# Second feed-forward block: gate and up projections as seven block products, interleaved with the down projection in three chunks

## The chip, the cores and the metric

The kernel runs on one core of a Trainium2 chip. The metric is the time of one execution in device microseconds (us), the median of three runs. The core has a matrix engine (TensorE, PE in the profile), a vector engine (VectorE, DVE), a scalar engine (ScalarE, ACT), GpSimd (POOL), and a queue (SyncE, SP) from which all loads and stores are issued here.

## The reference

One residual block on 512 tokens of width 1024, in float32: a half-step SwiGLU feed-forward block (FFN), a mixer of a gated DeltaNet group and a latent attention group, and a second half-step FFN. The change is in the second FFN, which computes

```
h  = rms(x) * (1 + scale) + shift            # scale and shift from the condition c, one per channel
gate, up = split(h @ w_in)                   # w_in: 1024 x 5632, so gate and up have 2816 columns each
x  = x + 0.5 * g * ((silu(gate) * up) @ w_out)   # w_out: 2816 x 1024
```

## The kernel before

Activations lie transposed: a tile has 128 channels on the partitions and 512 tokens in the free dimension. x is eight such tiles, `self.xT[0..7]`. Each number that goes through TensorE is split in a high part (rounded to the format fp32r) and a low part (the rest), and each product is three matmuls (`mm3`, L257 to L261): high weight by high data (L259), high weight by low data (L260), low weight by high data (L261).

Weights come in units (`unit`, L198): one load of 8 x 128 x 128 numbers (512 KB; 6 x 128 x 128, 384 KB, for the last part of a down column) into a raw tile `wr`, a cast on ScalarE into the high tile `wh` (L191) and a subtraction on VectorE into the low tile `wl` (L192). Each of the three kinds has four tiles (pool `wp`, `bufs=4`, L83). A tile is given out again when its last reader has finished. `plan_units` lists the units in order; `next_unit` hands out the next and starts one more.

Other tiles of 128 x 512 come from a pool of 56 slots. In PSUM, where TensorE writes, there are three accumulators from `acc` (named pa) and five from `aux` (named pb).

The second FFN is `ffn2` (L718). `first_units` does three units (gate and up of column tile 0, gate of column tile 1) in two halves of 256 tokens, since the normalised input h of the second half is still being made. After that each of the 22 column tiles takes a gate unit and an up unit of 24 matmuls of 512 tokens each (8 input tiles by three), and `glu` (L585) makes the product: Silu on ScalarE, a multiplication, a cast to the high part (L592) and a subtraction for the low part (L593). When all 22 are there, `down` (L645) makes the eight output tiles: 22 input tiles by three matmuls each, in three units, and adds the result to x (L652). The last output tile is done in two halves of 256 tokens. `store` transposes a finished tile back on TensorE (L712), copies it (L714) and writes it out.

The order of the work on TensorE is the order of the program. Where code runs under `in_order` (L131), every engine, SP and GpSimd included, executes its instructions in the order in which the program emits them.

The input h of the second FFN is made in `norm_half` and `modulate` (L439 to L457), per half of the tokens: a multiplication on VectorE (L452), an addition of the shift with rounding on ScalarE (L454), and the low part on VectorE (L446). The late pool (12 more slots, used by the first FFN's last results) is closed by `late_exit` at the very end.

Of the kernel before, what the change touches and what calls it, by code (L numbers as in the profile page):

```python
# [18 lines left out]
P = 128  # L19
# [8 lines left out]
KPARTS = ((0, 8), (8, 8), (16, 6))  # L28

# [48 lines left out]
class Block:  # L78
# [144 lines left out]
    def plan_units(self):  # L223
# [4 lines left out]
        def ffn(w1, w2, first, ts):  # L228
            for f in range(first, FT):
                cols(w1, f * P)  # L230
                cols(w1, DFF + f * P)
            for t in ts:
                for k0, n in KPARTS:
                    self.specs.append(lambda k0=k0, n=n, t=t: self.unit(w2[k0 * P:(k0 + n) * P, t * P:(t + 1) * P], n))

        ffn(ins["ffn1_w_in"][0], ins["ffn1_w_out"][0], 3, [*range(KT), KT - 2])
# [10 lines left out]
        ffn(ins["ffn2_w_in"][0], ins["ffn2_w_out"][0], 0, range(KT))  # L247
# [168 lines left out]

    def rstd_diag(self, v):

        return self.diag(self.rms_cols(v, v.shape[1], D))
# [52 lines left out]
    def norm_half(self, half, acc, j):  # L472
# [5 lines left out]
        for k in range(0, KT, 2):  # L478
            self.modulate(range(k, k + 2), ts, rb, self.mod[j + 1], self.mod[j])
            yield  # L480

    def first_units(self, n, nb, lead, marks):
# [5 lines left out]
        with self.matmuls_in_order(self.last_mm):  # L488
            for half in range(2):
                ts = slice(half * HALF, half * HALF + HALF)  # L490
                for at, (kt, i) in enumerate([(kt, i) for kt in range(KT) for i in range(n)] if half else first):
                    self.dense(ps[i], units[i], self.h, ts, kt, kt + 1)
# [152 lines left out]
    def down(self, act, gate, norm=None):  # L645

        nc = self.nc
        accum = self.slot(s="na") if norm else None
        full, ha, hb = slice(0, NT), slice(0, HALF), slice(HALF, NT)

        def finish(t, ts, p):
            nc.vector.scalar_tensor_tensor(out=self.xT[t][:, ts], in0=p[:, ts], scalar=gate[:, t:t + 1],  # L652
                                           in1=self.xT[t][:, ts], op0=ALU.mult, op1=ALU.add)
            if norm:
                self.square_in(t, ts, accum)
# [12 lines left out]
        last = KT - 2 if norm else KT - 1  # L668
        side = Side()
        if norm:  # L670
            side.add(self.ada_rest((2, 3), True))
        for t in range(last):
            if norm and t == 1:
                self.masks()
            for i, _ in enumerate(parts(t, full)):
                side.step((2, 1, 2)[i])
                if not norm and i == 1 and t > 0:
                    self.store(t - 1, range(NB))
        side.flush()
        if not norm:  # L680
            t = KT - 1
            units = [self.next_unit(ahead=0) for _ in KPARTS]
            for i, _ in enumerate(parts(t, ha, units)):
                if i == 1:
                    self.store(t - 1, range(NB))
            for i, _ in enumerate(parts(t, hb, units)):
                if i == 1:
                    self.store(t, range(2))
            self.store(t, range(2, 4))
            return None  # L690
# [27 lines left out]
    def ffn2(self, nb):  # L718
        act = []
        ps = self.first_units(3, nb, 2, (7, 18, 15))  # L720
# [1060 lines left out]
```

## Time and profile before

| | |
|---|---|
| three runs | 1093.94, 1094.52, 1096.87 us; median 1094.52 |
| span of the profiled execution | 1091.4 us (the page gives no other time of it; the median of the runs stands 3.1 us above) |
| busy over the span | TensorE 97%, VectorE 52%, ScalarE 35%, GpSimd 4% |
| mean granted TensorE clock | 0.989 of full speed |
| second FFN | its first matmul starts at 717.1 us; to the end |

The span runs from the first to the last instruction of one profiled execution. Matmuls are pipelined: one starts before the one ahead of it has ended, so their durations overlap and the distance of starts is what one costs. A line such as L191 or L259 belongs to a helper and stands for all its callers; the names of the tiles (`wh<-wr`, `pa<-hh,wh`) tell them apart. `x60` is a count, the number behind the busy time is the mean in ns, and behind the last bar stands the idle time of the engine ahead of these instructions with what ended it.

### The profile page before, as it was taken

Reading aid. Unit: us, or ns where it says so; the run is one execution under the profiler, and the core shown is the slowest. Engines: PE = TensorE matmul, PEld = TensorE weight load, DVE = VectorE, ACT = ScalarE, POOL = GpSimd, SP = SyncE. Lnnn points to the kernel's source line nnn. Section 1 sums busy time; section 2 is a strip of 40 time slices with the busy share of each in tenths; the row PEclk is TensorE's granted clock in tenths of the full one; section 3 lists DMA queues with packets and bytes.
Section 4 is the critical chain, followed back from the end, with each engine's and each line's share of the span. In section 5 each row is a group of like instructions: output and inputs, shape, how many; then the busy total and the mean of one; then the engine's idle time right before and its main releaser. Section 6 shows DMA issues by size and latency. Waiting matters only on the chain. (4 is left out here: it accounts for less than half of the span.)

```text
span 1091.4 us, 14122 instructions
## 1 busy us (share of the span) xinstructions
PE 1059.7 (97%) x5583; PEld 880.8 (81%) x5583; DVE 571.5 (52%) x1021; ACT 385.6 (35%) x636; POOL 43.2 (4%) x94
## 2 busy tenths in 40 slices
PE   6999999999999999998997999999999999999998
PEld 4778878788887899886776779988888888888887
DVE  4488884333687366388767545684333333322220
ACT  4242222222222235475565434443222222222220
POOL 1000000000000000001000021200000000000000
PEclk9999999999999999999999969999999999999999
DMA  9989963332796455221223001124333333334320
GB/s 275 268 244 302 295 202 97 96 97 87 241 289 218 115 127 151 59 58 39 59 54 82 6 20 40 39 78 116 97 97 97 97 97 97 92 97 115 97 72 30
DMA packets 210576, 132.04 MB, mean 121 GB/s; under 512 B 13633, under 2 KB 194638, under 8 KB 210510
## 3 DMA queue, kind: packets, MB, share of 16 engines
q1 hardware_dynamic: 210510, 131.14, 41.2%
q8 instruction: 44, 0.72, 0.3%
q14 instruction: 22, 0.18, 0.1%
HBM read 128.63 MB, written 2.49 MB: 120 GB/s over the span
## 5 line engine op out<-in xcount | busy, mean ns | idle before, releaser
L191 ACT CAST wh<-wr 128x1024 fp32r<-128x1024 f32 (+1 forms) x170 | 173.3, 1021 | 494.8 <-PE pa L260 338.3
L259 PE MATMUL pa<-hh,wh 128*128 128x512 f32 (+1 forms) x885 | 338.6, 383 | 5.5 <-ACT z L1597 4.3
L260 PE MATMUL pa<-hl,wh 128*128 128x512 f32 (+1 forms) x885 | 336.5, 380 | 3.3 <-DVE hl L446 3.2
L261 PE MATMUL pa<-hh,wl 128*128 128x512 f32 (+1 forms) x885 | 336.0, 380 | 0.0
L192 DVE TENSOR_TENSOR wl<-wr,wh 128x1024 fp32r<-128x1024 f32 (+1 forms) x170 | 201.5, 1186 | 237.5 <-ACT wh L191 231.4
L259 PEld LDWEIGHTS pa<-hh,wh 128*128 128x128 f32 x885 | 166.8, 188 | 40.5 <-ACT z L1597 4.7
L260 PEld LDWEIGHTS pa<-hl,wh 128*128 128x128 f32 x885 | 166.8, 188 | 34.7 <-DVE hl L446 4.6
L261 PEld LDWEIGHTS pa<-hh,wl 128*128 128x128 f32 x885 | 166.7, 188 | 30.8 <-DVE wl L192 0.4
L259 PE MATMUL pa<-ah,wh 128*128 128x512 f32 (+1 forms) x418 | 150.1, 359 | 0.0
L261 PE MATMUL pa<-ah,wl 128*128 128x512 f32 (+1 forms) x418 | 148.8, 356 | 0.0
L260 PE MATMUL pa<-al,wh 128*128 128x512 f32 (+1 forms) x418 | 148.6, 356 | 0.0
L259 PEld LDWEIGHTS pa<-ah,wh 128*128 128x128 f32 x418 | 79.0, 189 | 12.7 <-ACT wh L191 1.7
L261 PEld LDWEIGHTS pa<-ah,wl 128*128 128x128 f32 x418 | 79.0, 189 | 11.4
L260 PEld LDWEIGHTS pa<-al,wh 128*128 128x128 f32 x418 | 79.0, 189 | 11.0
L590 DVE TENSOR_TENSOR af<-sg,pa 128x512 f32<-128x512 f32 x40 | 27.5, 687 | 103.0 <-PE pa L261 102.9
L544 DVE SCALAR_TENSOR_TENSOR aa<-ar,sc,aa 128x512 f32<-128x512 f32 x98 | 73.2, 751 | 14.3 <-DMA ar<-in_w_ada 12.9
L652 DVE SCALAR_TENSOR_TENSOR xT<-pa,mod,xT 128x512 f32<-128x512 f32 (+1 forms) x19 | 12.7, 667 | 48.3 <-PE pa L261 48.3
L592 ACT CAST ah<-af 128x512 fp32r<-128x512 f32 x44 | 27.4, 622 | 19.3 <-DVE af L590 19.3
L259 PE MATMUL pa<-mh,wh 128*128 128x256 f32 (+1 forms) x96 | 32.6, 341 | 0.0
L260 PE MATMUL pa<-ml,wh 128*128 128x256 f32 (+1 forms) x96 | 32.3, 336 | 0.0
L261 PE MATMUL pa<-mh,wl 128*128 128x256 f32 (+1 forms) x96 | 32.0, 333 | 0.0
L593 DVE TENSOR_TENSOR al<-af,ah 128x512 fp32r<-128x512 f32 x44 | 30.2, 687 | 1.0 <-ACT ah L592 0.9
(350 smaller groups left out, 985.5 us busy)
## 6 DMA issues: line engine op xcount, KB each, us to landing
wr<-in_ffn_w_in SPq DMA_DIRECT2D x82, 512.0 KB, 3.9
ar<-in_w_ada SPq DMA_DIRECT2D x48, 512.0 KB, 6.6
wr<-in_ffn_w_out SPq DMA_DIRECT2D x34, 512.0 KB, 4.4
ar<-in_w_ada SPq DMA_DIRECT2D x48, 256.0 KB, 5.3
wr<-in_w_in SPq DMA_DIRECT2D x21, 512.0 KB, 3.8
wr<-in_ffn_w_out SPq DMA_DIRECT2D x17, 384.0 KB, 4.4
wr<-in_w_out SPq DMA_DIRECT2D x8, 512.0 KB, 5.0
wr<-in_ffn_w_in SPq DMA_DIRECT2D x8, 384.0 KB, 8.7
```

Source lines behind the costliest of these rows:

```text
L191: self.nc.scalar.copy(hi, raw)
L192: self.nc.vector.tensor_tensor(out=lo, in0=raw, in1=hi.bitcast(F32), op=ALU.subtract)
L259: mm(out, wh, xh, start=start, stop=False)
L260: mm(out, wh, xl, start=False, stop=False)
L261: mm(out, wl, xh, start=False, stop=stop)
L544: nc.vector.scalar_tensor_tensor(out=acc, in0=a, scalar=sc, in1=acc, op0=ALU.mult, op1=ALU.add)
L590: nc.vector.tensor_tensor(out=a, in0=s, in1=pu, op=ALU.mult)
L592: nc.scalar.copy(ah, a)
L593: nc.vector.tensor_tensor(out=al, in0=a, in1=ah.bitcast(F32), op=ALU.subtract)
L652: nc.vector.scalar_tensor_tensor(out=self.xT[t][:, ts], in0=p[:, ts], scalar=gate[:, t:t + 1], in1=self.xT[t][:, ts], op0=ALU.mult, op1=AL ...
```

## The change

The gate and the up projection of one column tile are together a product of two by two blocks: two halves of the input channels (4 tiles of 128 each) by two outputs (gate, up), times two halves of the tokens. That is eight block products of 4 x 128 channels by 256 tokens. Strassen's algorithm (in Winograd's form) makes it with seven, and with sums and differences of blocks. One block product is 4 channel tiles by three matmuls = 12 matmuls of 256 tokens.

- **Inputs.** h is kept in another layout: per channel tile and half of the tokens one slot with high and low part side by side (`self.B`), and the value ahead of the shift in `self.tm`. `modulate_forms` does the same operations as `modulate`. Four more sets of inputs, t1 to t4 (each 4 slots, one per channel tile of a half), are sums and differences of blocks of h, made once in `glu_forms`: eight calls, the first four with two VectorE operations of 128 x 256, two casts on ScalarE and two operations on GpSimd each, the last four with three on VectorE, two casts and one on GpSimd.
- **Weights.** Per pair of gate unit g and up unit u (each 128 x 1024, two halves A and B) four sums are made: x and y, each with halves A and B; half of them are on VectorE, half on GpSimd. Then u, x, y (1024 columns) and the B half of g (512) are split in high and low part. u and x use tiles of `wp` as before, y uses two tiles of its own (`ws`, opened after the late pool is closed), g's parts use slots.
- **Schedule.** The first `PLAIN` = 3 column tiles stay as they were, now all in halves of 256 tokens. The other 19 pairs run in steps: pair j has base 7j, and its seven products stand at base + 0 (up0), 1 (up1), 3 (s2), 4 (s3), 6 (s1), 9 (s4), 12 (gate1), so that each step has one product, of three pairs in turn. The other operations of a pair are tasks at fixed steps, emitted ahead of the product of the same step: load at base - 13, sums at -8 and -5, splits of u at -6 (cast) and -4 (subtraction), of x at -4 and -3, of y at -3 and -2, of g at -1 and 0; ScalarE copies of partial sums out of PSUM at 1, 4 and 7 (the accumulator A goes on being added to); then both 8, gate1's Silu 9, act1 11, gate0 (addition and Silu) 13, act0 (multiplication and cast) 15, act_low 16. Several pairs at one step are emitted with the oldest pair first. The tasks of steps -12 to -1 are emitted during the three plain units 3 to 5, four per unit, and `glu_forms` with the first eight of these.
- **Down.** The 22 rows of w_out are taken in chunks of 8, 8 and 6. Chunk one is begun at step 40, ahead of that step's tasks, by emitting units 0 and 1 (load, cast and subtraction of output tiles 0 and 1); at step 45, behind that step's tasks and ahead of its product, the whole chunk is emitted: for each of the eight output tiles the unit two tiles on, 24 matmuls of 512, and the addition to x. Chunk two does the same at steps 96 and 101. The load of the pair that falls in between is held until output tile 6. The last chunk follows the last pair, with parts of its first three output tiles between that pair's last products; the stores run in it.
- All of this after `first_units` is emitted under `in_order`. `late_exit` moves ahead of `ffn2`.

```diff
+PLAIN = 3
+STEPS = {0: "up0", 1: "up1", 3: "s2", 4: "s3", 6: "s1", 9: "s4", 12: "gate1"}
...
+    def mm_both(self, out, w, b, start, stop):
+        hi, lo = w
+        mm = self.nc.tensor.matmul
+        kw = dict(skip_group_check=True)
+        mm(out, hi, b[:, :HALF], start=start, stop=False, **kw)
+        mm(out, hi, b[:, HALF:], start=False, stop=False, **kw)
+        mm(out, lo, b[:, :HALF], start=False, stop=stop, **kw)
...
+    def glu_forms(self, k, which):
+        nc, v = self.nc, self.nc.vector
+        a, b = self.tm[k], self.tm[k + 4]
+        lo, hi = slice(0, HALF), slice(HALF, NT)
+        shift = self.mod[6][:, k + 4:k + 5]
+        if which == 0:
+            self.tv[k] = t = self.slot(s="tv")
+            nc.gpsimd.tensor_tensor(out=t[:, lo], in0=a[:, lo], in1=a[:, hi], op=ALU.subtract)
+            v.scalar_tensor_tensor(out=t[:, hi], in0=b[:, hi], scalar=shift, in1=t[:, lo], op0=ALU.add, op1=ALU.add)
+            names = ("t1", "t2")
+        else:
+            old, t = self.tv[k], self.slot(s="tv")
+            v.scalar_tensor_tensor(out=t[:, lo], in0=b[:, hi], scalar=self.dsh[:, k:k + 1], in1=a[:, hi], op0=ALU.add,
+                                   op1=ALU.subtract)
+            v.scalar_tensor_tensor(out=t[:, hi], in0=b[:, lo], scalar=shift, in1=old[:, hi], op0=ALU.add,
+                                   op1=ALU.subtract, reverse1=True)
+            names = ("t3", "t4")
+        for name, part, eng in zip(names, (lo, hi), (nc.gpsimd, nc.vector) if which == 0 else (nc.vector, nc.gpsimd)):
+            f = self.slot(F32R, "hf")
+            self.T[name].append(f)
+            nc.scalar.copy(f[:, lo], t[:, part])
+            eng.tensor_tensor(out=f[:, hi], in0=t[:, part], in1=f[:, lo].bitcast(F32), op=ALU.subtract)
+
+    def pair_tasks(self, f, base, add):
...
+        def sums():
+            tiles(("x", "y"), ("sx", "sy"), F32, 1)
+            v.tensor_tensor(out=r["y"][:, A], in0=r["g"][:, A], in1=r["g"][:, B], op=ALU.add)
+            nc.gpsimd.tensor_tensor(out=r["x"][:, A], in0=r["u"][:, A], in1=r["g"][:, A], op=ALU.add)
+
+        def sums2():
+            v.scalar_tensor_tensor(out=r["x"][:, B], in0=r["y"][:, A], scalar=-1.0, in1=r["u"][:, A], op0=ALU.mult,
+                                   op1=ALU.subtract)
+            nc.gpsimd.tensor_tensor(out=r["y"][:, B], in0=r["u"][:, B], in1=r["x"][:, B], op=ALU.subtract)
+
+        def hi(name, src, part=slice(0, 2 * NT)):
+            def go():
+                if name == "g1":
+                    r["g1h"], r["g1l"] = self.slot(F32R, "gh"), self.slot(F32R, "gl")
+                elif name == "y":
+                    tiles(("yh", "yl"), ("yh", "yl"), F32R, 2)
+                else:
+                    for e in "hl":
+                        r[name + e] = flat(self.wp.tile([P, 8, P], F32R, tag="w" + e, name=self.name("w" + e)))
+                nc.scalar.copy(r[name + "h"], r[src][:, part])
+            return go
...
+        def both():
+            r["cc"] = self.slot(s="cc")
+            v.tensor_tensor(out=r["cc"], in0=r["xp"], in1=r["BC"], op=ALU.add)
...
+        for at, go in ((-13, load), (-8, sums), (-5, sums2), (-6, hi("u", "u")), (-4, lo("u", "u")), (-4, hi("x", "x")),
+                       (-3, lo("x", "x")), (-3, hi("y", "y")), (-2, lo("y", "y")), (-1, hi("g1", "g", B)),
+                       (0, lo("g1", "g", B)), (1, early_copy("xp", L)), (4, early_copy("uc", L)), (7, early_copy("xp", H)),
+                       (8, both), (9, gate1), (11, act1), (13, gate0), (15, act0), (16, act_low)):
+            add(base + at, go)
...
+        def down(k0, m, held):
+            full = slice(0, NT)
+            units = [unit(t, k0, m) for t in range(2)]
+            yield
+            acts = self.act[k0:k0 + m]
+            for t in range(KT):
+                if t + 2 < KT:
+                    units.append(unit(t + 2, k0, m))
+                if t == KT - 2:
+                    for go in held:
+                        go()
+                p = self.acc()
+                self.dense(p, units[t], acts, full, 0, m, m - 1)
+                finish(t, full, p)
+
+        ends = {KPARTS[c][0] + KPARTS[c][1] - 1 - PLAIN: KPARTS[c] for c in range(2)}
+        stop = 7 * (n - 1)
+        waiting = None
+        for s in range(0, stop + 13):
+            i = (s - 12) // 7
+            if (s - 12) % 7 == 0 and i in ends:
+                at = 7 * (i + 4) - 13
+                held = [go for go in tasks.get(at, []) if go.__name__ == "load"]
+                tasks[at] = [go for go in tasks.get(at, []) if go not in held]
+                waiting = down(*ends[i], held)
+                next(waiting)
+            tick(s)
+            if waiting and (s - 17) % 7 == 0:
+                drain(waiting)
+                waiting = None
+            for j in range(n):
+                if s - 7 * j in STEPS:
+                    self.product(pairs[j], STEPS[s - 7 * j])
...
     nb = k.mixer(nb)
+    k.late_exit()
     k.ffn2(nb)
-    k.late_exit()
```

More of the change, by code (lines that the diff above doesn't have):

```diff
@@ L718, in ffn2 @@
     def ffn2(self, nb):
-        act = []
-        ps = self.first_units(3, nb, 2, (7, 18, 15))
-        act.append(self.glu(ps[0], ps[1]))
-        act.append(self.glu(ps[2], self.proj(self.aux())))
-        for f in range(2, FT):
-            pg = self.proj()
-            act.append(self.glu(pg, self.proj(), f >= 17))
-        self.down(act, self.mod[8])
+        with self.tc.tile_pool(name="ws", bufs=1) as self.ws:
+            ps = self.first_units(PLAIN, nb, 2, (7, 18, 15), True)
+            with self.in_order():
+                self.ffn2_rest(ps)
```

206 lines of the change are left out of this document (171 added, 35 removed).

## The prediction

> **What bounds the kernel now.** I read the page first, then the second FFN by windows, then its groups of instructions, then single instructions in order of time.
>
> ```profile
> span 1091.4 us, 14122 instructions
> PE 1059.7 (97%) x5583; PEld 880.8 (81%) x5583; DVE 571.5 (52%) x1021; ACT 385.6 (35%) x636; POOL 43.2 (4%) x94
> ...
> 760.00:1000.00 240.00, 240.00 (x1063) 198.76 (x1062) 79.46 (x85) 66.95 (x84) 0.00 (x0) 1.00 0.34 98
> ```
>
> From 760 to 1000 us TensorE has no gap, at clock 1.00, while VectorE works a third of the time and GpSimd not at all. So TensorE's instruction stream sets the time there, and the change has to be costed in matmuls first. A matmul's duration overlaps the next one, so I take the pitch, from the starts in the timeline (TensorE only), for the two widths:
>
> ```profile
> 1060.42 0.39 PE L259 MATMUL pa<-ah,wh 128*128 128x512 f32 x1
> ...
> 1065.63 0.39 PE L261 MATMUL pa<-ah,wl 128*128 128x512 f32 x1
> ...
> 731.05 0.28 PE L259 MATMUL pa<-hh,wh 128*128 128x256 f32 x1
> ...
> 739.57 0.28 PE L261 MATMUL pa<-hh,wl 128*128 128x256 f32 x1
> ```
>
> The first two are 24 matmuls of 512 columns: 5.21 / 23 = 0.2265 us each. The last two are 72 of 256 columns: 8.52 / 71 = 0.120 us. Half the width costs 53%, not 50%, of the full one.
>
> **The matmuls.** A gate and up pair was 2 x 8 x 3 = 48 matmuls of 512: 10.87 us. It becomes 7 products of 12 matmuls of 256: 84 x 0.120 = 10.08 us. Saved 0.79 x 19 pairs = 15.05 us. Three units of the plain pairs go from 72 matmuls of 512 (16.31) to 144 of 256 (17.28): +0.97. The last down tile was 132 of 256 (15.84) and becomes 48 of 512 and 36 of 256 (15.19): -0.65. Sum: **-14.7 us**, if TensorE never waits.
>
> The Trainium skill (TensorE: Matmul & The Clock Gate, Back-to-back issue gap) gives N/2.4 + 2.5 ns as the isolated gap, which is 109 ns for 256 and 216 ns for 512 columns. By it a pair would save 48 x 0.216 - 84 x 0.109 = 1.2 us, some 22.5 us over 19 pairs; the trace's 120 and 226.5 ns disagree and decide.
>
> **What feeds the products.** Durations from the groups by form, 705 us to the end, and GpSimd's groups of the whole run:
>
> ```profile
> L192 DVE TENSOR_TENSOR wl<-wr,wh 128x1024 fp32r<-128x1024 f32 x60 | 73.5, 1225 | 106.3 <-ACT wh L191 102.7
> L191 ACT CAST wh<-wr 128x1024 fp32r<-128x1024 f32 x60 | 63.1, 1053 | 210.8 <-PE pa L260 131.0 <-issue 79.7
> L593 DVE TENSOR_TENSOR al<-af,ah 128x512 fp32r<-128x512 f32 x22 | 15.1, 686 | 0.0
> L592 ACT CAST ah<-af 128x512 fp32r<-128x512 f32 x22 | 13.7, 623 | 0.0
> L652 DVE SCALAR_TENSOR_TENSOR xT<-pa,mod,xT 128x512 f32<-128x512 f32 x7 | 5.3, 751 | 20.3 <-PE pa L261 20.3
> L470 DVE TENSOR_TENSOR na<-na,sq 128x256 f32<-128x256 f32 x7 | 3.0, 424 | 0.0
> L436 ACT COPY rb<-pb 128x256 f32<-128x256 f32 x2 | 0.7, 363 | 2.3 <-PE pb L434 2.3
> ...
> L882 POOL TENSOR_TENSOR kd<-ktk,kcd 128x512 f32<-128x512 f32 x3 | 3.1, 1038 | 0.0
> ```
>
> VectorE per pair: three subtractions of 1024 (3.68), five operations of 512 (5 x 0.69 = 3.43, one of them a scalar_tensor_tensor, +0.06), three of 256 (1.27): 8.4 us. ScalarE: three casts of 1024 (3.16), two of 512 (1.25), five operations of 256 (about 1.9): 6.3 us. GpSimd: 2 x 1.04. All are under the 10.08 us of TensorE, so seven steps of 1.44 us a round hold, with VectorE at 83% instead of about a third. I cost the steady rounds at nothing; the 2 us of GpSimd are added below as a rival. The DMA bytes are the same. The mixer's end issues the same operations in another layout: nothing. Closing the late pool earlier issues no work.
>
> **The entry, +6.5 us.** In the 12 quarters (17.3 us) of the three plain units VectorE must do two gated units, two weight splits, eight calls of glu_forms and pair 0's sums and first split, in a fixed order. By the rows: 2 x 1.4, 2 x 1.22, 20 operations of 256 (8.5), then 0.69, 0.75 and 1.22: 16.4 us, and within each glu_forms VectorE waits for ScalarE's copy, itself behind VectorE's result (some 0.4 us, eight times), and for GpSimd. Unit 5's cast stands on ScalarE behind glu of the second pair, at about 11.7 us, where TensorE wants it at 11.5: with cast and subtraction some 2 us late. Product up0 of pair 0 wants its low part at 17.3 + 2, and has it at about 24: 4.5 us. Bounds: 0 (VectorE keeps up) and 11 (every GpSimd operation blocks VectorE).
>
> **The hand-over to a down chunk.** At step 40 (pair 6 is next) the code emits two units of w_out, load, cast and subtraction, ahead of everything else of step 40, on queues whose order is pinned. The raw tiles of weights (wr) are four. Pair 6's g is read until step 42 and pair 7's two until 49 and 45, so one is free: unit 0 takes it, and unit 1 can load only when unit 0's subtraction has ended. That such a load waits for this subtraction shows in SP's waits (740 to 1090 us), and a load's time in the DMA issues of that stretch:
>
> ```profile
> SPq L116 <- DVE wl L192: 277.2, 56, 16.5
> ...
> wr<-in_ffn_w_out SPq DMA_DIRECT2D x16, 512.0 KB, 4.3
> ```
>
> The walk, from the start of step 40: pair 6's u is free about 2.4 us earlier, so unit 0 lands at 1.9; cast to 3.0, subtraction to 4.2; unit 1's load lands at 8.5; cast to 9.6, subtraction to 10.8. Behind it on VectorE: pair 6's last split (12.1), gate0's addition of pair 4 (12.5); on ScalarE gate0's Silu (13.0), a cast of 512 (13.6), and then the copy of pair 5's partial sum (14.0). Product s4 of pair 5 overwrites that sum at step 44, due at 5.8. So TensorE stands **8.2 us**. Bounds: 6.5 (unit 0 already landed) and 10.5 (two GpSimd operations more ahead).
>
> Does such a gap cost clock? In the windows around the one place where TensorE was thinly used (and, from the timeline, where dense matmuls resume there):
>
> ```profile
> 638.00:640.00 2.00, 2.00 (x12) 1.26 (x10) 0.89 (x4) 0.68 (x3) 2.00 (x3) 0.58 0.04 8
> 640.00:642.00 2.00, 2.00 (x20) 1.32 (x21) 0.35 (x2) 0.22 (x1) 0.48 (x1) 0.50 0.00 0
> ...
> 651.19 0.79 PE L261 MATMUL pa<-mh,wl 128*128 128x512 f32 x1
> ...
> 652.00:654.00 2.00, 2.00 (x6) 1.52 (x6) 1.89 (x2) 0.00 (x0) 0.00 (x0) 0.50 0.00 0
> 654.00:656.00 2.00, 2.00 (x12) 1.75 (x11) 0.57 (x1) 0.00 (x0) 0.00 (x0) 0.65 0.39 114
> 656.00:658.00 2.00, 2.00 (x18) 1.91 (x17) 0.72 (x2) 0.48 (x1) 0.00 (x0) 1.00 0.52 156
> ```
>
> The clock falls to 0.50 and comes back some 3.4 us after dense matmuls resume (651.2 to about 654.6). At half speed that is **1.7 us** after the stall; bounds 0 and 3.4.
>
> **Inside a down chunk.** The high tiles (wh) are four too. When the chunk runs, at step 45, three are held: pair 6's x (until step 46, behind the chunk), pair 7's u (step 43) and pair 7's x (step 45, emitted just ahead of the chunk; it takes unit 0's tile after the first of eight output tiles). Units 2 to 7 share the one that is left: each cast waits until the output tile before it has finished. That release, cast and subtraction as they follow now:
>
> ```profile
> 1039.07 0.39 PE L260 MATMUL pa<-al,wh 128*128 128x512 f32 x1
> 1039.30 0.39 PE L261 MATMUL pa<-ah,wl 128*128 128x512 f32 x1
> 1039.50 1.06 ACT L191 CAST wh<-wr 128x1024 fp32r<-128x1024 f32 x1 [3.25 <-PE pa L260]
> 1039.53 0.39 PE L259 MATMUL pa<-ah,wh 128*128 128x512 f32 x1
> ...
> 1040.59 1.23 DVE L192 TENSOR_TENSOR wl<-wr,wh 128x1024 fp32r<-128x1024 f32 x1
> ```
>
> The cast begins at about the time the next matmul could (1039.50 against 1039.53); today that matmul uses a unit cast long before. In the chunk it is its own unit: two matmuls can start after 1.06 us, the third after 1.06 + 1.23 = 2.3 us, where it was due after 0.45. 1.85 us x 6 = **11.1 us**. Bounds: 6.4 (the subtraction hidden) and 14.4 (2.4 each, nothing overlapped). ScalarE and VectorE have no other work there that could cover it.
>
> Per chunk 8.2 + 1.7 + 11.1 = 21.0, and chunk two (steps 96 to 101) has the same lifetimes: 42.0. The third chunk comes when no pair needs new weights: four tiles free, cost nothing beyond the count above.
>
> **Sum**: -14.7 + 6.5 + 42.0 = +33.8: a span of 1091.4 + 33.8 = 1125.2. The median of the runs, 1094.5, stands 3.1 above the profiled span; I take the same around the new one: **1128.3 us**.
>
> **Rivals.**
> 1. The hand-overs are hidden (faster): tiles come free earlier than I count, or the casts run ahead into the chunk. For it: today's casts run units ahead (131.0 us of their idle time is for a free tile). Against: three tiles are held by name. Then 1094.5 - 14.7 + 6.5 = 1086.3, and 1079.8 without the entry's stall.
> 2. Only one of the two stalls: with the load's alone 1094.5 - 8.2 + 2 x 9.9 = 1106.1; with the tiles' alone 1108.5.
> 3. VectorE becomes the bound of the rounds, through GpSimd. Around 634 us:
>
> ```profile
> 634.00 1.04 POOL L882 TENSOR_TENSOR kd<-ktk,kcd 128x512 f32<-128x512 f32 x1
> 634.07 1.52 DVE L882 TENSOR_TENSOR on<-ao,ry 128x512 f32<-128x512 f32 x1 [1.12 <-POOL ry L177]
> 635.00 1.49 POOL L882 TENSOR_TENSOR kbg<-ktk,eG 128x512 f32<-128x512 f32 x1
> ```
>
> VectorE's 0.69 takes 1.52 beside GpSimd's 1.04: one after the other. If both operations a pair cost VectorE in full, 8.4 + 2.1 = 10.5, and with 0.9 for waits on ScalarE 11.4 against 10.08: +1.3 x 19 = 25 us on top, 1153. Against it: VectorE's three operations on PSUM and its waits can take up GpSimd's time.
>
> That exclusive lock is what the Trainium skill states (SBUF — State Buffer, SBUF: two separate sides) for a VectorE operation with two SBUF inputs; by its rule the sum would be this rival's, and the three rows above agree with the rule.
>
> **Chances.** Forecast 0.60; rival 1 0.18; rival 2 0.13; rival 3 0.09. A change under 0.3% (3.3 us) can't be told from none. Rival 1 is faster by more than that; the others slower; 0.04 for small sums between. Faster 0.18, same 0.04, slower 0.78. The forecast's own bounds are -14.7 + 0 + 2 x 12.9 = +11.1 and -14.7 + 11 + 2 x 28.3 = +52.9, all bad cases together; the range 1100 to 1145 holds most of these and rival 2.
>
> **What would show it.** TensorE's pitch 0.120 in the products; two dense stretches of about 55 us instead of 43.5, with ScalarE's casts in them released by TensorE and TensorE waiting for cast and subtraction; ahead of each a gap of about 8 us ending with ScalarE's copy, and a clock dip; no regular wait in the rounds. A TensorE without gaps there would make the forecast wrong by 40 us.

## The result, and the profile after

The changed kernel takes 1140.29 us (median of four runs, 1136.85 to 1142.76); beside it the kernel before took 1094.23 us. The ratio is 1.0416, with a 95% interval of 1.0393 to 1.0440: slower by 4.2%. The forecast was 1128.3 us, in a range of 1100 to 1145.

The page of the kernel after, its first rows (busy time, share of the span, instructions):

```profile
span 1141.0 us, 15960 instructions
PE 1067.8 (94%) x6291; PEld 914.1 (80%) x6291; DVE 695.3 (61%) x1191; ACT 440.9 (39%) x766; POOL 122.9 (11%) x144
```

And two stretches of it by windows (length, then busy time and instructions of PE, PEld, DVE, ACT, POOL, then granted clock, DMA share, GB/s):

```profile
760.00:1000.00 240.00, 210.43 (x1450) 195.50 (x1449) 156.54 (x186) 97.85 (x162) 59.60 (x34) 0.94 0.31 90
900.00:960.00 60.00, 60.00 (x502) 60.00 (x502) 53.89 (x67) 33.45 (x60) 20.04 (x12) 1.00 0.34 98
```

TensorE, which had no gap from 760 to 1000 us before, is now idle for 30 of these 240 us. But between the two down chunks (900 to 960) it has none. So the seven products themselves run as planned. The time is lost at a few places, and the waits of TensorE name them (from 715 us to the end; total, times, longest):

```profile
PE pb L444 <- ACT xp L823: 18.4, 3, 8.1
PE pa L262 <- ACT wh L193: 11.0, 12, 1.0
PE pa L264 <- DVE wl L194: 6.3, 12, 0.5
PE pb L737 <- DVE xT L917: 3.8, 5, 1.4
PE pa L444 <- DVE xT L2004: 2.9, 1, 2.9
PE pb L446 <- DVE wl L816: 2.5, 1, 2.5
PE pa L444 <- ACT wh L193: 1.4, 1, 1.4
PE pa L446 <- DVE wl L194: 0.8, 1, 0.8
PE pa L262 <- DVE xT L917: 0.6, 1, 0.6
```

Before, the same question has four rows with 2.7 us in all. Now two hand-overs of about 8 us and twelve output tiles with two waits each make up most. The rest lies at the entry (from the plain units to pair 0's products) and at the end (the last chunk and the stores).

The second FFN starts with its first matmul at 717.14 us before and at 718.64 after. Though the work ahead of it is the same but for the layout of h, this start lies between 716.43 and 722.28 us in the profiled executions of all the kernels below. So beside the medians I compare the *FFN time*, from that matmul to the end of the span: 1091.4 - 717.1 = 374.3 us before, 1141.0 - 718.6 = 422.4 after, **+48.1**. This is one execution of each kernel (the medians differ by 46.1). How far it can be trusted, the entry shows: the six kernels below with the entry unchanged (the kernel after and experiments 1, 2, 3, 4 and 6) reach the twelfth product of the pairs 68.74 to 68.88 us behind the first matmul. From the starts in the timeline the loss adds up so:

| place | predicted | measured |
|---|---|---|
| fewer matmul columns | -14.7 | -14.7 by the pitch (55 products between the chunks take 79.2 us: 12 x 0.120 each) |
| entry (plain units, pair 0) | +6.5 | +12.6 |
| two hand-overs, with the clock lost behind them | 2 x 9.9 | 2 x 10.3 (8.0 of waiting, 2.2 of clock) |
| two chunks, output tiles 2 to 7 | 2 x 11.1 | 2 x 12.0 (7.45 us from tile to tile, 5.44 without the waits) |
| last chunk and stores | 0 | +5.5 |
| sum | +33.8 | +48.0 |

The hand-over, step by step, from the timelines of the three engines in the kernel after (start, duration, engine, operation, idle time ahead of it and what ended it):

```profile
828.94 1.05 ACT L193 CAST wh<-wr 128x1024 fp32r<-128x1024 f32 x1 [2.48 <-DMA wr<-in_ffn_w_out]
830.02 1.23 DVE L194 TENSOR_TENSOR wl<-wr,wh 128x1024 fp32r<-128x1024 f32 x1 [3.78 <-ACT wh L193]
...
835.16 1.04 ACT L193 CAST wh<-wr 128x1024 fp32r<-128x1024 f32 x1 [5.17 <-DMA wr<-in_ffn_w_out]
836.24 1.23 DVE L194 TENSOR_TENSOR wl<-wr,wh 128x1024 fp32r<-128x1024 f32 x1 [4.99 <-ACT wh L193]
837.38 1.22 DVE L816 TENSOR_TENSOR yl<-sy,yh 128x1024 fp32r<-128x1024 f32 x1
838.51 0.41 DVE L833 TENSOR_TENSOR uc<-uc,pb 128x256 f32<-128x256 f32 x1
...
838.96 0.42 ACT L834 ACTIVATE uc<-uc 128x256 f32<-128x256 f32 x1 [2.76 <-DVE uc L833]
839.28 0.60 ACT L811 CAST gh<-wr 128x512 fp32r<-128x512 f32 x1
839.79 0.36 ACT L823 COPY xp<-pb 128x256 f32<-128x256 f32 x1
...
840.21 0.58 PE L444 MATMUL pb<-hb,yh 128*128 128x256 f32 x1 [7.97 <-ACT xp L823]
```

This is the walk of the prediction: unit 0 lands, is cast and subtracted (to 831.2), only then unit 1 is loaded, lands at 835.1, and the copy that TensorE waits for stands seventh behind it. Counted from the start of step 40 (826.3 us), unit 0 lands at 2.6 us where the walk had 1.9, unit 1 at 8.8 (8.5), and the copy is done at 13.8 (14.0). Inside the chunk, ScalarE's casts are released by TensorE and TensorE waits for them:

```profile
855.77 0.50 PE L262 MATMUL pa<-ah,wh 128*128 128x512 f32 x1 [0.95 <-ACT wh L193]
...
857.03 0.50 PE L264 MATMUL pa<-ah,wl 128*128 128x512 f32 x1 [0.53 <-DVE wl L194]
...
862.13 1.04 ACT L193 CAST wh<-wr 128x1024 fp32r<-128x1024 f32 x1 [6.41 <-PE pa L263]
```

### The profile page after: what moved, and what is told of

Read it like the earlier page. It is cut to its first block, busy times and chain, and to the rows that moved or that the text cites. A ratio compares the mean times of both kernels' runs of the same rounds, so it can differ in the third digit from the quotient of the medians.

```text
span 1141.0 us, 15960 instructions
## 1 busy us (share of the span) xinstructions
PE 1067.8 (94%) x6291; PEld 914.1 (80%) x6291; DVE 695.3 (61%) x1191; ACT 440.9 (39%) x766; POOL 122.9 (11%) x144
## 5 line engine op out<-in xcount | busy, mean ns | idle before, releaser
L194 DVE TENSOR_TENSOR wl<-wr,wh 128x1024 fp32r<-128x1024 f32 (+1 forms) x132 | 154.7, 1174 | 220.9 <-ACT wh L193 218.5
L262 PE MATMUL pa<-hh,wh 128*128 128x512 f32 (+1 forms) x517 | 200.7, 388 | 4.3 <-ACT z L1861 4.3
L263 PE MATMUL pa<-hl,wh 128*128 128x512 f32 (+1 forms) x517 | 198.4, 384 | 1.4 <-DVE hl L483 1.4
L264 PE MATMUL pa<-hh,wl 128*128 128x512 f32 (+1 forms) x517 | 198.5, 384 | 0.0
L262 PEld LDWEIGHTS pa<-hh,wh 128*128 128x128 f32 x517 | 98.2, 190 | 25.9 <-ACT z L1861 4.7
L263 PEld LDWEIGHTS pa<-hl,wh 128*128 128x128 f32 x517 | 98.3, 190 | 19.1 <-DVE hl L483 1.7
L264 PEld LDWEIGHTS pa<-hh,wl 128*128 128x128 f32 x517 | 98.0, 190 | 18.7 <-DVE wl L194 0.4
L264 PEld LDWEIGHTS pa<-ah,wl 128*128 128x128 f32 x402 | 76.2, 190 | 23.3 <-DVE wl L194 11.5
L446 PE MATMUL pb<-hb,wl 128*128 128x256 f32 x152 | 43.8, 288 | 2.5 <-DVE wl L816 2.5
L444 PE MATMUL pb<-hf,wh 128*128 128x256 f32 x152 | 43.9, 289 | 2.3 <-ACT xp L823 2.3
L444 PE MATMUL pb<-hb,wh 128*128 128x256 f32 x152 | 43.8, 288 | 0.0
L445 PE MATMUL pb<-hf,wh 128*128 128x256 f32 x152 | 43.7, 288 | 0.0
L445 PE MATMUL pb<-hb,wh 128*128 128x256 f32 x152 | 43.6, 287 | 0.0
```

What stands on the lines that cost most here:

```text
L194: self.nc.vector.tensor_tensor(out=lo, in0=raw, in1=hi.bitcast(F32), op=ALU.subtract)
L262: mm(out, wh, xh, start=start, stop=False)
L263: mm(out, wh, xl, start=False, stop=False)
L264: mm(out, wl, xh, start=False, stop=stop)
L444: mm(out, hi, b[:, :HALF], start=start, stop=False, **kw)
L445: mm(out, hi, b[:, HALF:], start=False, stop=False, **kw)
```

## The experiments

Each is an edit of the kernel after (the later ones are edits on top, as named). Medians are beside the kernel before, which stood at 1092.5 to 1094.4 us; the ratio with its interval is to that kernel. "Less" of an FFN time is against the kernel after, where nothing else is named.

**1. The chunks two steps later.**

```diff
-                waiting = down(*ends[i], held)
+                start, waiting = s, down(*ends[i], held)
...
-            if waiting and (s - 17) % 7 == 0:
+            if waiting and s == start + 7:
```

> Each of the two down chunks that lie between the pairs is put two steps later (step 47 and 103 in place of 45 and 101), nothing else. By then pair 6's x is no longer read and two high tiles of weights are left in place of one. My theory (the chunk's units 2 to 7 wait for the one tile that is left): the tiles inside a chunk start 5.4 us apart in place of 7.45, ScalarE's casts there no longer start behind the last matmul of the tile before, 12 x 2.0 = 24 us less: 1140 - 24 = 1116 us; the 8-us gap ahead of each chunk stays. Rival, the units are bound by their transfers or by VectorE: the tiles stay 7.4 us apart and the time at 1140 us. Second rival, the time saved comes back behind the chunk, since pair 8's weights are loaded only in the chunk's last two tiles and its first sums now stand one step behind it and not three: a new gap of up to 4 us a chunk, 1124 us.

Measured: 1117.15 us, ratio 1.0212 (1.0171 to 1.0253). FFN time 397.3, 25.1 less. The chunk takes 43.55 us (850.23 to 893.78) in place of 56.4. TensorE's waits between 780 and 1060 us are one row, where the kernel after has also those for `wh` and `wl`:

```profile
PE pb L444 <- ACT xp L823: 16.0, 2, 8.3
```

The twelve pairs of waits are gone and the two hand-overs are as they were; nothing came back behind the chunk. The expectation was wrong in one point: the casts still start when an output tile has ended (at 861.15, 866.55 us and so on). But with one more tile free each is for the unit after the one that starts then, so TensorE no longer stands for it. The tile that was missing caused the waits in the chunk.

**2. Transfers at step 40, splits later.** `raw_unit` is the load of a unit, `split_raw` its cast and subtraction; what is between the `yield`s is emitted two and four steps after the load.

```diff
-            units = [unit(t, k0, m) for t in range(2)]
-            yield
+            raws = [raw_unit(t, k0, m) for t in range(2)]
+            units = []
+            for t in range(2):
+                yield
+                units.append(split_raw(raws[t], m))
+            yield
...
+            if waiting and (s - 12) % 7 in (2, 4):
+                next(waiting)
```

> At step 40 only the two transfers of a chunk's first two units are issued; their cast and subtraction are emitted two and four steps later, and the chunk stays at step 45. My theory (TensorE's 8-us gap is ScalarE and VectorE standing behind unit 1's transfer, which itself waits for unit 0's subtraction): both gaps of 8.1 us and the half-speed matmuls behind them (1.3 us each) go: 2 x 9.4 = 18.8 us less, 1140 - 19 = 1121 us, and no row of TensorE at the hand-over names the copy of the partial sum. The 7.45 us between the tiles of a chunk stay. Rival, the queues are so full there that the copy is late in any place: the gap shrinks to the cast and subtraction of one unit, some 2 to 3 us, 1130 us. Rival, the wait only moves to the chunk's start, where unit 1's subtraction is then late: 4 us a chunk come back, 1129 us.

Measured: 1121.33 us, ratio 1.0256 (1.0210 to 1.0302). FFN time 401.1, 21.3 less. The complement of the first experiment, again all waits of TensorE between 780 and 1060 us:

```profile
PE pa L262 <- ACT wh L193: 10.9, 12, 0.9
PE pa L264 <- DVE wl L194: 6.3, 12, 0.5
```

The hand-over costs nothing now, neither wait nor clock. The transfers are still emitted at step 40; what had cost the time was the order in which ScalarE and VectorE stood behind them.

**3. Both.**

> Both edits: the chunks two steps later, and the first two units' cast and subtraction two and four steps behind their transfers. My theory has the two stalls independent, so the gains add: 24 + 19 = 43 us less, 1140 - 43 = 1097 us, within some 3 us of the kernel before the change (1094). TensorE then has no wait of over 0.5 us from the first pair's hand-over to the last pair. Rival, the two have a common cause (ScalarE's or VectorE's total work around a chunk): the gains don't add, 1110 us or more.

Measured: 1098.87 us (ten runs), ratio 1.0040 (1.0018 to 1.0062). FFN time 377.7, 44.7 less; the two alone give 25.1 + 21.3 = 46.4. From 780 to 1060 us no wait of TensorE is left. The gains add to within 2 us, so the two stalls are separate. In the table above they are 44.6 of the 62.7 us lost; the rest, 18.1 us at the entry and the end, is 3.4 us more than the 14.7 us that the fewer columns save, and by that much the FFN time of this kernel still lies above that of the kernel before.

**4. Room of its own for unit 1.** How much of the hand-over hangs on unit 1's transfer waiting for unit 0's subtraction? Here unit 1 is loaded into two free slots (`three` is the two in the shape of half a weight tile each), one half after the other.

```diff
-            units = [unit(t, k0, m) for t in range(2)]
+            units = [unit(0, k0, m)]
+            raws = [self.slot(s="w5") for _ in range(2)]
...
+            for q, r in enumerate(three):
+                self.load(r, w2[(k0 + 4 * q) * P:(k0 + 4 * q + 4) * P, P:2 * P].rearrange("(k p) f -> p k f", p=P))
+            for q, r in enumerate(three):
+                self.split_w(r, hi[:, 4 * q:4 * q + 4, :], lo[:, 4 * q:4 * q + 4, :])
```

> The kernel after the change, with one thing altered: at each hand-over the second unit of the down chunk is loaded into room of its own (two free tiles of 128x512, a transfer of 256 KB and a cast and subtraction of 512 columns for each half) in place of the fourth weight tile, so its transfer no longer waits for the first unit's subtraction. The casts and subtractions stay where they were. My theory (about half of the 8.1-us gap is this one missing tile, the rest is the first unit's transfer and the two splits ahead of the copy): the second unit lands some 4.4 us earlier, the gap shrinks to 3.5 to 4 us, 2 x 4.4 = 8.8 us less, 1132 us. Rival (the two transfers are bound by each other, or the queue's order by something else): the gap stays at 8 us, 1140 us. Rival, the whole gap hangs on the tile: it goes, 1121 us.

Measured: 1127.82 us, ratio 1.0333 (1.0276 to 1.0390). FFN time 410.9, 11.5 less. ScalarE no longer waits between the two units:

```profile
827.74 1.05 ACT L193 CAST wh<-wr 128x1024 fp32r<-128x1024 f32 x1 [2.74 <-DMA wr<-in_ffn_w_out]
828.69 1.34 ACT L193 CAST wh<-w 128x512 fp32r<-128x512 f32 x2
```

And of TensorE's waits between 780 and 1060 us the row of the hand-over is

```profile
PE pb L444 <- ACT xp L823: 6.5, 2, 3.3
```

The two gaps are 3.2 and 3.3 us in place of 8.0 and 8.1. So 4.8 us of each hung on the one missing tile; 3.2 remain for unit 0's transfer and the splits ahead of the copy. Both kinds of cure work: room for the transfer cures 60%, the later place of the splits all of it.

**5. The entry in another order.** Units 4 and 5 are split ahead of `glu_forms`; `form_step` begins one of its calls and ends the one before; pair 0's u is split two quarters earlier:

```diff
-            p, u = self.acc(), self.next_unit(ahead=1 if i + 1 < 2 * PLAIN else 0)
+            p, u = self.acc(), self.next_unit(ahead=2 * PLAIN - 1 - i)
...
-                    if forms:
-                        forms.pop(0)()
+                    form_step()
```

> Only the entry is reordered: the cast and subtraction of the plain units 4 and 5 stand ahead of the sums of the activations, each of these eight calls has its last half emitted behind the first half of the next one, pair 0's first split is emitted two quarters earlier, and the last gated unit ahead of pair 1's first sums. The work is the same. My theory (TensorE's 12.6 us of waits and low clock between unit 3 and pair 0 come from the order in which VectorE and ScalarE stand behind each other, the rows of the trace sum to about 17.8 us of VectorE's work for 21 us): 8 to 12 us less, 1130 us (1128 to 1132). Rival, VectorE and GpSimd simply have too much to do there, beside each other: the waits move to other rows and at most 4 us are won, 1136 us or more.

Measured: 1139.97 us (1131.34 to 1142.50), ratio 1.0404 (1.0349 to 1.0458). FFN time 418.9, 3.5 less: the rival. The waits of the plain units are gone, but the third product of pair 0 now waits 5.6 us for the copy of its partial sum, where it waited 2.3. I took that for an order again (the copy stood behind the cast of the last gated unit) and tried once more:

```diff
+        early = lambda at, go: add(at - 2 if -8 <= at <= -2 else at, go)
+        pairs = [self.pair_tasks(PLAIN + j, 7 * j, add if j else early) for j in range(n)]
...
+        forms = [(5 * e + k - 12, self.glu_forms(k, e)) for e in range(2) for k in range(4)]
...
+        add(1, lambda: self.act.append(self.glu(last, prev)))
```

> The entry again, with what the first reordering showed: there the plain units ran without a wait, but pair 0's first product stood 1.6 us for VectorE's low part and its third 5.6 us for ScalarE's copy of the partial sum, which stood behind the cast of the last gated unit. Now all of pair 0's sums and splits are emitted two quarters earlier, the forms t3 and t4 begin one quarter later, and the last gated unit is emitted behind that copy, at pair 0's step 1. My theory (the order, not the amount of work): 10 to 12.6 us less than 1140, 1129 us, and no wait over 1 us between unit 3 and the first hand-over. Rival (VectorE and GpSimd have too much to do in these 23 us): a wait of 4 to 6 us for a form or for the split of pair 0's x or y takes its place, 1134 us.

Measured: 1138.50 us (1130.20 to 1140.62), ratio 1.0391 (1.0355 to 1.0426). FFN time 419.3, 3.1 less. Missed again. The rival was right in the size of the wait and not in its place: it is again the copy that came 5.1 us late, behind ScalarE's casts of the forms, and these had waited 1.9 us twice for VectorE. What kept VectorE is in its groups by form, 741 to 768 us in this kernel:

```profile
L759 DVE SCALAR_TENSOR_TENSOR tv<-tm,mod,tv 128x256 f32<-128x256 f32 x4 | 3.8, 975 | 0.0
L763 DVE SCALAR_TENSOR_TENSOR tv<-tm,dsh,tm 128x256 f32<-128x256 f32 x4 | 3.3, 828 | 0.0
L765 DVE SCALAR_TENSOR_TENSOR tv<-tm,mod,tv 128x256 f32<-128x256 f32 x4 | 2.9, 734 | 0.0
```

Operations that the prediction put at 0.42 us each take 0.73 to 0.98 in the mean where GpSimd works beside them. VectorE is busy for 12.93 of the 13 us from 754 to 767, so what is late there depends on what is put ahead of it.

**6. The end.** The transfers of the last chunk's units 4 to 7 ahead of the stores:

```diff
+        raws = [raw_unit(t, k0, m) for t in range(4, 7)]
         for t in range(KT):
+            if t == 1:
+                raws.append(raw_unit(7, k0, m))
+            if t and raws:
+                units.append(split_raw(raws.pop(0), m))
...
-            if 4 <= t + 2 < KT and t >= 2:
-                units.append(unit(t + 2, k0, m))
```

> Only the last chunk is edited: the transfers of its units 4 to 7 are issued ahead of the stores (three before the first output tile, one behind the first), and each cast and subtraction stands ahead of the tile that runs meanwhile; in the kernel after the change each of these transfers stands on SyncE behind a store. My theory (the 5.5 us that the end lost come from ScalarE's casts waiting some 4.1 us each for these transfers, VectorE's subtraction and then its addition to the residual behind them, and the transposes behind that): 4 to 5.5 us less, 1140 - 5 = 1135 us, and no transpose waits for the addition by more than 0.5 us. Rival, the addition alone (0.75 us behind a tile's last matmul) is what the transposes wait for, in any order: 1140 us.

Measured: 1138.68 us (1135.95 to 1142.78), ratio 1.0410 (1.0381 to 1.0438). By the medians that is not to be told from 1140.29; the FFN time is 418.2, 4.2 less, and the row that named the loss (`PE pb L737 <- DVE xT L917: 3.8, 5, 1.4`) has become, behind 1040 us,

```profile
PE pb L737 <- DVE xT L927: 0.4, 1, 0.4
```

So the transposes waited for the addition, and it for a subtraction behind a transfer that SyncE had issued after a store: in the kernel after, ScalarE's casts behind 1060 us wait four times for these transfers, 16.6 us in all.

**7. All edits so far together** (3, the second entry, 6).

> All edits at once: the chunks two steps later, their first two units split behind the transfers, the second reordering of the entry, and the last chunk's transfers ahead of the stores. My theory has all the stalls apart from each other, so TensorE's stream should decide again: 1098.9 (the two chunk edits together) - 11 - 5 = 1083 us, which is near 1094.4 - 14.7 of fewer matmul columns and 3 us above it. That is faster than the kernel before. Rival, less of the matmul saving is real than the 14.7 us (the pitch of the narrow matmuls or the clock costs it): 1090 us or more with a TensorE that has no gap.

Measured: 1091.81 us (twelve runs), ratio 0.9979 (0.9958 to 1.0001): level with the kernel before. FFN time 372.8, 1.5 below. Not the 1083 forecast, since the entry had not given what the forecast put down for it (3 in place of 11).

**8. The pairs' sums on VectorE**, on top of 3:

```diff
-            nc.gpsimd.tensor_tensor(out=r["x"][:, A], in0=r["u"][:, A], in1=r["g"][:, A], op=ALU.add)
+            v.tensor_tensor(out=r["x"][:, A], in0=r["u"][:, A], in1=r["g"][:, A], op=ALU.add)
...
-            nc.gpsimd.tensor_tensor(out=r["y"][:, B], in0=r["u"][:, B], in1=r["x"][:, B], op=ALU.subtract)
+            v.tensor_tensor(out=r["y"][:, B], in0=r["u"][:, B], in1=r["x"][:, B], op=ALU.subtract)
```

> The two chunk edits, and the two sums per pair that GpSimd makes are made by VectorE instead, in the same places. It tells how near VectorE is to being the bound of the rounds, and what GpSimd's help is worth. With GpSimd, VectorE is busy 9.06 us of 10.08 a pair (two of its subtractions take 0.70 and 0.54 us longer than alone). Without, the rows give 8.4 + 2 x 0.69 = 9.8 us. My theory: that still fits, TensorE keeps its 1.44 us a product and the time stays at 1099 us (within 3). Rival, VectorE's waits on ScalarE (about 0.9 us a pair) come on top, 10.7 against 10.08: 0.6 x 16 rounds = 10 us more, 1109 us, with regular waits of TensorE for a subtraction.

Measured: 1096.51 us (ten runs), ratio 1.0015 (0.9997 to 1.0033). FFN time 375.3, 2.4 below that of 3, all of it at the entry (the third product of pair 0 starts 53.1 us behind the first matmul in place of 55.7). The rounds keep 1.44 us a product. What it says of GpSimd stands in windows of five pairs, first with GpSimd's sums (the kernel of experiment 3), then without:

```profile
890.00:940.40 50.40, 50.40 (x422) 50.40 (x422) 45.38 (x56) 28.24 (x51) 18.05 (x11) 1.00 0.36 105
```

```profile
890.00:940.40 50.40, 50.40 (x423) 50.40 (x422) 44.87 (x66) 28.52 (x51) 0.00 (x0) 1.00 0.36 105
```

VectorE does ten operations more and is busy for half a microsecond less. GpSimd's two sums cost VectorE all that they save: the two subtractions that they make longer take 1.24 us more a pair (1921 and 1765 ns in place of 1225, in the kernel after), and the sums themselves would be 2 x 0.69 = 1.38.

**9. The entry by due times**, on top of 7 and 8: forms t3 first, t4 at pair 0's steps 3 to 7, the last gated unit at step 5.

```diff
+        forms = [((-12, -7, 3)[e] + k, self.glu_forms(k, e)) for e in range(3) for k in range(4)]
...
+        add(5, lambda: self.act.append(self.glu(last, prev)))
```

> All edits again with a third order of the entry and the pairs' two sums on VectorE. In the second order VectorE was busy without a break from 754 to 767 us: it made the forms t4 (needed only by pair 0's seventh product) ahead of the rest, and many of its 0.40-us operations took 0.88 us beside GpSimd. Now each form t3 is made first, the forms t4 at pair 0's steps 3 to 7 and the last gated unit at step 5; the pairs' sums are VectorE's as in the run before. My theory now (VectorE's amount of work ahead of pair 0's third product, GpSimd's share of it included, sets the entry): the third product starts some 46 us behind the first matmul of the FFN in place of 51.5, the loss of clock behind the stall goes too, and the time falls by 5 to 7 us from 1091.8: 1086 us, faster than the kernel before by 0.7%. Rival, the waits only move to the next product (s3, which needs all four t3): 2 us or less, 1090 us.

Measured: 1089.55 us (twelve runs), ratio 0.9969 (0.9953 to 0.9985). The third product starts 46.2 us behind the first matmul, as forecast; the FFN time is 369.6, 3.2 less than in 7, half of the forecast, because the third product still waited 2.5 us and s4 then 1.8, each for a copy, and TensorE ran at half clock behind them. By the medians the gain is 2.3 us, nearer to the rival's 1090 than to 1086. Beside it, with GpSimd's twelve operations of the forms on VectorE as well:

```diff
-        pool = nc.gpsimd
+        pool = v
```

> As the kernel beside it, but the twelve operations of 128x256 of the forms t1 and t4 that GpSimd makes are VectorE's too, so GpSimd does nothing in this stage. VectorE gets 12 x 0.40 = 4.8 us more to do; if GpSimd's operations hold VectorE up for their whole length (each neighbour takes 0.88 in place of 0.40 us: 12 x 0.48 = 5.8 us), it gets 5.8 less: no difference or 1 us faster, 1085 us. Rival, GpSimd's work is for free where VectorE waits for ScalarE or PSUM: 3 to 5 us slower, 1090 us.

Measured: 1088.58 us (twelve runs), ratio 0.9970 (0.9955 to 0.9985), FFN time 368.9: no clear difference, as the theory has it. The group that took 975 ns above is now

```profile
L766 DVE SCALAR_TENSOR_TENSOR tv<-tm,mod,tv 128x256 f32<-128x256 f32 x4 | 1.9, 485 | 0.1
```

**10. The copy first**, on top of that.

```diff
-        early = lambda at, go: add(at - 2 if -8 <= at <= -2 else at, go)
+        early = lambda at, go: add(at - 2 if -8 <= at <= -3 else at + 2 if at in (-1, 0) else at, go)
...
+        tasks[1].insert(0, tasks[1].pop(1))
...
-        add(5, lambda: self.act.append(self.glu(last, prev)))
+        add(10, lambda: self.act.append(self.glu(last, prev)))
```

> As the kernel without GpSimd, with the two waits left at the entry taken up (the third product of pair 0 stood 2.5 us, its s4's counterpart in the next round 2.4 us, both for ScalarE's copy of the partial sum): the low part of pair 0's y comes behind the forms t3, the copy ahead of the cast of its g, the split of g two steps later, the last gated unit at step 10 in place of 5. My theory (ScalarE's order again, with VectorE now just fast enough): both waits under 1 us and no clock lost behind them: 5 to 7 us less than 1088.6, 1083 us. Rival, VectorE is still behind and the next product waits: 1 to 2 us less, 1087 us.

Measured: 1086.62 us (twelve runs, 1078.12 to 1093.12), ratio 0.9941 (0.9911 to 0.9971). FFN time 367.3. A gain of about 2 us in place of 5 to 7, so nearer to its rival: the third product waits 0.9 us, but s1 waits 2.1 for the other copy (`uc`), and the clock is lost behind that one. Still this is below both kernels: by 0.6% (0.3 to 0.9) below the one before, by 4.7% below the one after.

## Why the prediction was right, and where it was not

**Right in sign and in its two chief mechanisms, 12 us too low.** The forecast's case happened: two dense stretches of 56.4 us, ahead of each a gap of 8 us that ends with ScalarE's copy, no wait in the rounds. Hand-overs and chunks were put at 42.0 us and measured 44.6. The terms together missed by 14.2 us (33.8 against 48.0), nearly all of it at the entry and the end. That the median missed by no more than 12 is chance: 3.1 us were added for its distance above the profiled span, and here it lies 0.7 below it.

- *The matmuls, -14.7.* The best kernel bears it out. Its FFN time is 7.0 us below that of the kernel before, and by its starts it still loses 6.6 at the entry (0.43 in the plain units, 1.04 ahead of the third product, 5.12 from there to the first chunk); 7.0 + 6.6 = 13.6, so all but 1 us is there.
- *The rounds, nothing.* Right: 55 products in 79.2 us. VectorE's price was a little low, 9.06 us of 10.08 a pair (45.28 us in five pairs) against 8.4.
- *The hand-over, 8.2 and 1.7.* Measured 8.0 and 2.2. The clock was misread: a mean of 0.65 from 654 to 656 us is half clock up to 655.4, not 654.6, so 4.2 us behind the resume at 651.2 and 2.1 us lost, which is what came. Experiment 4 shows that its chief part is the raw tile, as the walk had it, and experiment 2 that the order behind it is what lets it reach TensorE.
- *The chunk, 6 x 1.85.* Measured 6 x 2.0; experiment 1 shows that the held tiles are the cause.
- *The entry, +6.5.* Here the term failed; 12.6 lies above its own upper bound of 11. The waits alone are 1.4 + 0.8 + 2.5 + 2.3 = 7.0 us, so their sum came near by luck: unit 5's 2.2 us are as said (about 2), but pair 0's low part was 2.5 late and not 4.5, and the 2.3 us for the copy of pair 0's partial sum were not in the walk. Another 5.6 went in matmuls at half clock. I had priced the clock only behind the 8-us gaps, and the list of VectorE's operations with their durations alone, though the rival's rows showed 1.52 in place of 0.69 us beside GpSimd.
- *The end, 0.* The other term that failed, +5.5: free tiles were counted, but not that the loads of units 4 to 7 are emitted behind stores on one queue. Experiment 6 shows it for 4.2 of the 5.5.

**The rivals.** Rivals 1 and 2 fall with the waits above: both stalls were there in full. Rival 3, VectorE bound through GpSimd, is wrong for the rounds, where 1 us of VectorE's time a pair was still free, but its mechanism is real: there it takes from VectorE what GpSimd was to save. It doesn't explain the entry alone, since with no GpSimd work left there (experiment 10) 6.6 us are still lost. Two groups of VectorE between 900 and 970 us in the kernel after show it, where the same operation takes 1225 ns alone:

```profile
L816 DVE TENSOR_TENSOR yl<-sy,yh 128x1024 fp32r<-128x1024 f32 x7 | 13.4, 1921 | 3.1 <-ACT yh L811 3.1
L816 DVE TENSOR_TENSOR wl<-sx,wh 128x1024 fp32r<-128x1024 f32 x7 | 12.4, 1765 | 0.0
```

The Trainium skill (SBUF — State Buffer, SBUF: two separate sides) calls the port pair that the two engines share an exclusive lock. The longer operations here and experiments 8 and 9 agree: VectorE's time is about the same with GpSimd's help and without.

## What to carry to other kernels

A change that saves matmuls is to be checked for the places where its work is handed over: count, step by step, how many tiles of each pool are free when a new stream of weights begins, and what a pinned queue makes wait behind the first transfer. Emit a transfer early and its cast and subtraction only when it will have landed, and start a dense stretch when the tiles of the work before it are released; here these two edits of a few lines won 44.7 us, where the whole change had cost 48.1. Work given to GpSimd beside a VectorE that subtracts and adds tiles, as here, is to be priced as VectorE's own work.

## What was not expected of the hardware

**The clock falls after much shorter gaps than the prediction's, and not every time.** In the kernel after, TensorE waits 1.4 us, runs two matmuls or so, waits 0.8 us, and then runs at half clock. In the kernel of experiment 3 the same two waits cost no clock. And in experiment 4 the gap of 3.2 us is followed by clock 1.00, that of 3.3 us by 0.50. Behind the 8-us gaps it was 0.50 each time.

The traces show why. The granted clock changes only at places that lie multiples of 3.41 us apart: in the kernel after it falls at 755.94 us, rises at 759.35, falls at 766.18 and rises at 769.59. So here are windows that begin and end at such places (the second number is TensorE's busy time, the clock is the third from the end). First the kernel after, then experiment 3, then the two gaps of experiment 4:

```profile
752.52:755.93 3.41, 1.31 (x9) 0.90 (x8) 2.47 (x4) 1.56 (x2) 0.00 (x0) 1.00 0.00 0
755.94:759.35 3.41, 3.38 (x16) 3.38 (x17) 3.33 (x6) 1.20 (x3) 2.12 (x2) 0.50 0.53 154
```

```profile
754.69:758.10 3.41, 2.51 (x21) 2.31 (x20) 2.14 (x4) 2.43 (x5) 0.82 (x2) 1.00 0.00 0
758.11:761.52 3.41, 2.17 (x16) 1.96 (x17) 3.08 (x6) 1.24 (x3) 0.41 (x1) 1.00 0.13 36
761.53:764.93 3.40, 3.40 (x31) 3.40 (x30) 3.40 (x6) 0.92 (x3) 2.54 (x3) 1.00 0.39 117
```

```profile
829.06:832.47 3.41, 1.72 (x15) 1.52 (x13) 3.41 (x5) 0.87 (x2) 0.00 (x0) 1.00 0.33 100
832.48:835.89 3.41, 1.89 (x14) 1.85 (x15) 2.88 (x6) 2.26 (x6) 0.00 (x0) 1.00 0.21 61
835.90:839.30 3.40, 3.40 (x17) 2.79 (x16) 2.03 (x3) 1.08 (x2) 2.15 (x1) 1.00 0.51 150
...
969.01:972.42 3.41, 1.49 (x13) 1.28 (x11) 3.41 (x5) 0.72 (x2) 0.00 (x0) 1.00 0.37 111
972.43:975.83 3.40, 2.03 (x9) 2.04 (x10) 2.87 (x6) 2.40 (x6) 0.00 (x0) 0.50 0.22 65
```

A window with 2.1 or 1.9 us of idle time is followed by half clock; windows with 0.9, 1.2, 1.7 and 1.5 us are not. The gap of 3.2 us lay across two windows and that of 3.3 mostly in one. In all fourteen traces, from the start of the second FFN on, each window at full clock with more than 1.78 us idle is followed by 0.50, and none with less than 1.76. So what counts here is whether TensorE idles for about half of a window, and the same waits fall into the windows differently from kernel to kernel. The clock comes back behind a window with almost no idle time (0.47 us at most).

The Trainium skill (TensorE: Matmul & The Clock Gate, What's actually happening) has the clock fall after an idle window of about 3.4 us, with windows that run freely. The length and the free run agree with these traces. But the window need not be idle throughout: 1.9 us of idle time in it were enough, and there the measurement decides.

**GpSimd's help was worth nothing to VectorE**, neither for the pairs' sums (experiment 8) nor for the forms (9): 18.05 us of work on an engine that is otherwise idle left VectorE 0.5 us busier over the five pairs. Without GpSimd's part of the forms VectorE does twelve operations more in the whole run and is busy for 693.8 us in place of 694.8.
